# Opening two chunks of a feed-forward block side by side, without a plain first chunk, in a macaron encoder

## Chip, cores and metric

One core of a Trainium2 chip runs the whole program. The metric is the device time of one execution in microseconds (us), as the median of several runs; before the change it is 2751.84 us. A profile of one execution shows when each engine works: PE (TensorE, matmuls and transposes), DVE (VectorE), ACT (ScalarE), POOL (GpSimd, here mostly an issuer of DMAs that add to their target) and SP (SyncE, issuer of the loads).

## The reference

Two layers run over 768 tokens of 1024 features (a batch of 512 and one of 256). Each layer is a macaron block: half a feed-forward network, a token mixer, half a feed-forward network.

```python
def rmsnorm(x, g):
    xf = x.astype(F32)
    y = xf * lax.rsqrt(jnp.mean(xf * xf, axis=-1, keepdims=True) + NORM_EPS)
    return (y * g.astype(F32)).astype(x.dtype)

def swiglu_ffn(x, w1, w2):
    gate, up = jnp.split(x @ w1, 2, axis=-1)
    return (jax.nn.silu(gate) * up) @ w2
...
        x = x + 0.5 * swiglu_ffn(rmsnorm(x, norm_g[li, 0]), ffn_w1[li, 0], ffn_w2[li, 0])
        h = rmsnorm(x, norm_g[li, 1])
...
        x = x + mix
        x = x + 0.5 * swiglu_ffn(rmsnorm(x, norm_g[li, 2]), ffn_w1[li, 1], ffn_w2[li, 1])
    return rmsnorm(x, final_norm_g)
```

The first layer's mixer is a gated linear recurrence (hgrn), the second's is windowed attention (swa). The hidden width of the feed-forward network is 2816, that is 22 chunks of 128.

## The kernel before

**Stages.** f0, hgrn, f1, f2, swa, f3: four feed-forward blocks f0 to f3 and two mixers. f1 starts out of hgrn's output projection, f2 directly out of f1's last down product, f3 out of swa's projection.

**Numbers.** The matmuls work on pairs of high and low parts (`hi`, `lo`, of a type of fewer bits): a product of two values is three matmuls, hi by hi, hi by lo, lo by hi. The part `hi` is a cast by ACT, `lo` is the difference by DVE (`split`, lines 238 and 239 for weights, 383 and 384 for activations).

**Tokens in two halves.** The 768 tokens are two halves of 384 (H). A norm works on a block of 128 tokens: ACT squares and sums it (L433), takes the root (L434), DVE takes the reciprocal and scales the block (L435, L436). `turn` then transposes three blocks at a time by PE (L475) and ACT copies the result out of PSUM with the norm's weight (L478). There are four such groups of transposes for each norm: two parts of the features (part 0 and 1) for each half of the tokens. The quarters are called b00, b10, b01, b11 (part, half).

**A chunk.** The up projection of one chunk (gate and up columns) by all tokens is either plain, `up_plain`: 2 x 2 x 8 products, 96 matmuls of 128x384; or a Strassen pair, `up_pair`: seven products p1 to p7 of four steps, 84 matmuls. In a pair each product has its own operand: p1 takes b01, p2 b11, p3 b10, and p4 to p7 take the sums s4, s3, s2, s1 of the quarters, which DVE makes (`first_sum`, `up_sums`) and ACT and DVE split. Each product also has its own weight out of the four raw blocks of 128x512 of a chunk: single blocks for p1, p2, p4, and sums for the others, made partly by POOL's adding DMAs (`into`, L160) in separate `s3` tiles.

**The opening of a block.** While a norm's second half is still being made, a block of f1 to f3 starts with chunk 0 plain and chunk 1 as `opened_pair`, which takes its products in the order p7, p3, p1, p2, p6, p5, p4 and yields control so that the plain matmuls of the second half stand between. Block f0 has two plain chunks. From chunk 2 on every chunk is `up_pair`.

**Order and buffers.** Weights are planned in a queue: SP loads raw blocks into four `wr` slots (`load_next`, L175), ACT and DVE split them (`stage_next`), and `ahead` does so one product before PE needs it, within a bound of staged tiles (`GATED` while a block's first operands are missing). Work that belongs to the norms (`turn`, the sums) is put in `deferred` and run by `run_later` at set places. Each engine executes its own queue in order: an instruction that waits holds up all that stand behind it. A last down product (`down_last`) adds PE's results to x and calls the next norm for each block as soon as its two column halves are ready.

## Time and profile before

| | value |
|---|---|
| median of 3 runs | 2751.84 us (2751.36 to 2751.96) |
| profiled execution | 2752.12 us |
| its span in the trace | 2750.3 us |
| POOL busy | 470.8 us (17%) |
| DMA, mean | 124 GB/s |
| matmuls of a pair's products (L669) | 6972 |
| f1's opening | from 1022.20 us in the span |
| f2's opening | from 1508.17 us |
| f3's opening | from 2258.71 us |

The span is what the trace covers; the execution's own time is some 2 us more. Busy time of an engine over the whole span is an average over stages. Of PE, a row's duration overlaps the next, so the spacing of starts gives its pace. The chain of waits is followed back from the last instruction to what released each.

### The profile page before, as it was taken

What the parts mean: (1) busy time and instruction counts of PE and PEld (TensorE: products, weight loads), DVE (VectorE), ACT (ScalarE), POOL (GpSimd) and SP (SyncE); (2) the same over time, 40 slices, a digit from 0 to 9 for tenths busy, and PEclk for the clock granted to TensorE, in tenths of its full rate; (3) what the DMA queues carried; (4) which work ended last, traced back from release to release, by engine and by line L of the source; (5) the groups of instructions that cost most, each with busy time, mean ns of one, the idle gap of its engine ahead of it and who ended that gap; (6) DMA issues with size and microseconds to landing.
All of it is one profiled execution on the core that took longest, in us unless ns stands there. A gap on an engine that the chain in (4) does not pass through costs nothing.

```text
span 2750.3 us, 41122 instructions
## 1 busy us (share of the span) xinstructions
PE 2736.6 (99%) x15071; PEld 2544.4 (93%) x15071; DVE 2194.6 (80%) x3790; ACT 1407.9 (51%) x2664; POOL 470.8 (17%) x534
## 2 busy tenths in 40 slices
PE   9999999999999999999999999999999999999998
PEld 9999999989999889999998999999888889999997
DVE  8788788767877789788878987887847869788877
ACT  6344444634454676444455643444458855444444
POOL 1111121200000111211121121112005621211120
PEclk9999999999999999999999999999999999999999
DMA  6554556741122755655455565545424435655453
GB/s 176 128 127 115 124 145 166 223 144 38 40 56 68 199 132 126 146 134 129 117 135 138 115 149 129 130 115 142 130 74 114 87 76 121 142 134 131 115 135 111
DMA packets 363002, 340.70 MB, mean 124 GB/s; under 512 B 15320, under 2 KB 275376, under 8 KB 362800
## 3 DMA queue, kind: packets, MB, share of 16 engines
q1 hardware_dynamic: 306944, 227.18, 28.0%
q0 software_dynamic: 51552, 97.41, 20.4%
q10 hardware_dynamic: 4304, 13.49, 1.4%
q8 instruction: 118, 1.93, 0.3%
q14 instruction: 84, 0.69, 0.1%
HBM read 228.45 MB, written 15.73 MB: 89 GB/s over the span
## 4 chain that ended last, share of the span: by engine, by line
PE 94%; DMA 2%; DVE 1%; ACT 1%; issue 1%; POOL 0%; SPq 0%; ACTq 0%; POOLq 0%; DVEq 0%
PE ps L669 44%; PE ps L778 17%; PE ps L811 6%; PE ps L379 5%; PE ps L380 5%; PE ps L378 5%; PE ps L994 5%; PE ps L1057 3%; PE ps L475 1%; PE ps L1162 1%; PE ps L1676 1%; PE ps L1138 1%; PE ps L1638 0%; PE ps L1639 0%; PE ps L1688 0%
## 5 line engine op out<-in xcount | busy, mean ns | idle before, releaser
L669 PE MATMUL ps<-big,w 128*128 128x384 f32 x6972 | 1213.2, 334 | 0.0
L669 PEld LDWEIGHTS ps<-big,w 128*128 128x128 f32 x6972 | 1209.5, 188 | 1.4
L238 ACT CAST w<-wr 128x512 fp32r<-128x512 f32 (+1 forms) x615 | 430.0, 706 | 663.4 <-PE ps L669 336.0
L239 DVE TENSOR_TENSOR w<-wr,w 128x512 fp32r<-128x512 f32 (+1 forms) x541 | 435.8, 809 | 141.8 <-ACT w L238 115.1
L778 PE MATMUL ps<-w,big 128*128 128x512 f32 x2016 | 461.1, 390 | 0.0
L778 PEld LDWEIGHTS ps<-w,big 128*128 128x128 f32 x2016 | 376.6, 188 | 80.5 <-ACT big L383 2.7
L160 POOL DMA_DIRECT2D s<-wr x135 | 118.8, 890 | 1228.1 <-DVE wr L245 278.4
L841 DVE SCALAR_TENSOR_TENSOR x<-ps,x 128x512 f32<-128x512 f32 x420 | 273.0, 683 | 11.5 <-PE ps L811 11.2
L384 DVE TENSOR_TENSOR big<-tA,big 128x384 fp32r<-128x384 f32 x308 | 187.9, 621 | 20.9 <-ACT big L383 20.6
L160 POOL DMA_DIRECT2D wr<-wr x115 | 101.7, 885 | 537.9 <-DVE big L384 142.9
L383 ACT CAST big<-tA 128x384 fp32r<-128x384 f32 x308 | 152.8, 514 | 75.5 <-DVE tA L703 29.8
L378 PE MATMUL ps<-big,w 128*128 128x384 f32 x544 | 187.3, 345 | 0.1
L379 PE MATMUL ps<-big,w 128*128 128x384 f32 x544 | 183.1, 337 | 0.2 <-DVE big L455 0.2
L380 PE MATMUL ps<-big,w 128*128 128x384 f32 x544 | 182.6, 336 | 0.3 <-DVE w L384 0.3
L994 PE MATMUL ps<-w,big 128*128 128x512 f32 x756 | 178.2, 393 | 0.1
L811 PE MATMUL ps<-w,big 128*128 128x512 f32 x756 | 174.7, 391 | 0.9 <-DVE x L841 0.9
L811 PEld LDWEIGHTS ps<-w,big 128*128 128x128 f32 x756 | 141.0, 188 | 31.1 <-DVE x L841 2.0
L994 PEld LDWEIGHTS ps<-w,big 128*128 128x128 f32 x756 | 140.3, 188 | 29.0 <-DVE w L384 0.6
L239 POOL TENSOR_TENSOR w<-wr,w 128x512 fp32r<-128x512 f32 x74 | 107.4, 1452 | 81.0 <-ACT w L238 73.4
L245 DVE TENSOR_TENSOR wr<-wr,wr 128x512 f32<-128x512 f32 (+1 forms) x120 | 114.8, 956 | 0.4 <-DVE w L239 0.4
L384 DVE TENSOR_TENSOR w<-wr,w 128x1024 fp32r<-128x1024 f32 (+1 forms) x74 | 88.2, 1198 | 30.3 <-ACT w L383 29.1
L383 ACT CAST w<-wr 128x1024 fp32r<-128x1024 f32 (+1 forms) x74 | 75.7, 1029 | 70.1 <-PE ps L379 35.7
(251 smaller groups left out, 3698.5 us busy)
## 6 DMA issues: line engine op xcount, KB each, us to landing
wr<-in_ffn_w_dram SPq DMA_DIRECT2D x254, 512.0 KB, 4.0
s<-wr POOLq DMA_DIRECT2D x135, 256.0 KB, 4.7
s<-in_ffn_w_dram SPq DMA_DIRECT2D x126, 256.0 KB, 3.2
wr<-wr POOLq DMA_DIRECT2D x86, 256.0 KB, 4.1
wr<-in_hg_w_in_dram SPq DMA_DIRECT2D x32, 512.0 KB, 3.9
wr<-wr POOLq DMA_DIRECT2D x29, 512.0 KB, 4.7
spill<-x ACTq DMA_DIRECT2D x12, 512.0 KB, 4.0
kept<-big POOLq DMA_DIRECT2D x8, 768.0 KB, 6.1
```

Source lines behind the costliest of these rows:

```text
L238: nc.scalar.copy(h, src)
L239: (eng or nc.vector).tensor_sub(l, src, h.bitcast(F32))
L378: nc.tensor.matmul(out, a[0], b[0], start=first, stop=False)
L379: nc.tensor.matmul(out, a[0], b[1], start=False, stop=False)
L380: nc.tensor.matmul(out, a[1], b[0], start=False, stop=last)
L383: self.last_hi = self.nc.scalar.copy(hi, src).ins
L384: self.last_lo = self.nc.vector.tensor_sub(lo, src, hi.bitcast(F32)).ins
L669: self.nc.tensor.matmul(ps, a[x], b[y], start=first and k == 0 and i == 0, stop=k == 3 and i == 2, skip_group_check=True,)
L778: nc.tensor.matmul(ps, a[x], w[y], start=name == chain and kp == 0 and q == 0, stop=kp == 1 and q == 2, skip_group_check=True,)
L811: nc.tensor.matmul(ps, a[x], w[y], start=name == chain and k == 0 and q == 0, stop=k == 2 and q == 2, skip_group_check=True,)
L841: self.nc.vector.scalar_tensor_tensor(x, ps, c, x, ALU.mult, ALU.add)
L994: nc.tensor.matmul(ps, x[:, sl], y, start=fresh and k == 0 and q == 0, stop=k == 3 and q == 2, skip_group_check=True,)
```

## The change

Three settings and the code of the opening change, in f1, f2 and f3 alone:

- No plain chunk (`PLAIN` 0). Chunks 0 and 1 are both opened pairs and run side by side, product by product: p3 of chunk 0, p3 of chunk 1, then p7, p1, p2, p6, p5, p4 likewise.
- Half 0 is turned part 1 first, since p3 needs b10 and s1 needs both; b00 itself is no longer split, since no product takes it.
- The weights of both chunks are planned as one entry ("open") of eight raw blocks of 128x512 in four `wr` slots. The second chunk's two sum tiles are in a tile of the activations' pool (`big`), since there are only two `s3` tiles. Up to eight staged weight tiles may wait for the first operands (`GATED` 4).
- In the last down product ahead of a norm, `half_square` squares one half of a block's columns (of the first three blocks after p2, of the others after p5) and puts the sum through a scale and the epsilon; `norm_block` then squares the other half only and takes the root with the first as its bias.

```diff
-PLAIN = {"f0": 2, "f1": 1, "f2": 1, "f3": 1}
-GATED = 2
+PLAIN = {"f0": 2, "f1": 0, "f2": 0, "f3": 0}
+GATED = 4
...
-OPEN = ("p1", "p2", "p7", "p3", "p6", "p5", "p4")
+OPEN = ("p3", "p7", "p1", "p2", "p6", "p5", "p4")
...
+        if how == OPEN:
+            both = [self.quad_steps((key[0], i), raws[2 * i : 2 * i + 2], srcs[2 * i : 2 * i + 2], how) for i in range(2)]
+            steps = [step for pair in zip(*both) for step in pair]
+            inuse = lambda left: 4 if left > 5 else 3 if left == 5 else min(left, 2)
+            self.loaded.append((steps, inuse))
+            return
...
+        spot = self.big([P, 2, 512]) if order == OPEN and key[1] else None
         for i, src in enumerate(three):
-            t = self.wp.tile([P, 512], F32, tag="s3", name=self.name("s3"), bufs=2)
+            if spot is None:
+                t = self.wp.tile([P, 512], F32, tag="s3", name=self.name("s3"), bufs=2)
+            else:
+                t = spot[:, i]
...
+    def half_square(self, b, c):
+        nc = self.nc
+        xn, r = self.big([P, D]), self.stat(1)
+        sl = slice(c * 512, c * 512 + 512)
+        nc.scalar.activation(xn[:, sl], self.x[b][:, sl], AF.Square, accum_out=r)
+        nc.scalar.activation(r, r, AF.Identity, bias=self.eps, scale=1.0 / D)
+        self.ready[b] = xn, r, slice(512 - c * 512, D - c * 512)
+
     def norm_block(self, b, vector=False):
         nc = self.nc
+        if b in self.ready:
+            xn, bias, sl = self.ready.pop(b)
+            r = self.stat(1)
+            nc.scalar.activation(xn[:, sl], self.x[b][:, sl], AF.Square, accum_out=r)
+            nc.scalar.activation(r, r, AF.Sqrt, bias=bias, scale=1.0 / D)
...
-        if half == 0 and part == 0:
+        if half == 0 and part == int(row in (2, 3, 5)):
...
-                self.put(f"b{part}{half}", kp, self.tn[(part, half)][:, kp])
+                if part or half or row < 2:
+                    self.put(f"b{part}{half}", kp, self.tn[(part, half)][:, kp])
...
-        self.later(lambda: self.turn(half, 0, row), lambda: self.turn(half, 1, row))
+        parts = (1, 0) if not half and row in (2, 3, 5) else (0, 1)
+        self.later(*(lambda part=part: self.turn(half, part, row) for part in parts))
...
-        pair = self.opened_pair(tag, 1)
-        pss = self.up_plain(tag, 0, 0, iter(()), ((3,), (0, 3)))
-        next(pair)
-        ts[0] = self.gated(pss, self.last_hi, self.last_lo)
+            return ts
+        pairs = [self.opened_pair(tag, j) for j in range(2)]
+        self.run_later()
+        for name in OPEN:
+            for j, pair in enumerate(pairs):
+                out = next(pair)
+                if (name, j) in (("p7", 0),):
+                    self.run_later()
+                elif (name, j) == ("p7", 1):
+                    self.run_later(len(self.deferred))
+                if name == "p4":
+                    for half, t in out:
+                        ts[2 * j + half] = t
+                        if (j, half) != (0, 1):
+                            put(f"b{j}{half}", t, 0)
...
+                elif name == "p5":
+                    self.half_square(HB + i, 1)
+                elif name == "p2" and next_row is not None:
+                    self.half_square(i, 0)
```

How the instructions stand on three engines where f2 opens, before and after (numbers behind a name tell tiles apart; they differ between the two programs).

POOL's adding DMAs ahead of f2's first products, before. The chunk of the opened pair has the raw blocks `wr_1894` and `wr_1895` and the two sum tiles `s3_1896` and `s3_1897`:

```order
L160 DMA s3_1896_13425<-wr_1894_13421 128x512
L160 DMA s3_1897_13428<-wr_1894_13421 128x512
L160 DMA wr_1895_13423<-wr_1895_13423 128x512
L160 DMA s3_1897_13428<-wr_1895_13423 128x512
L160 DMA wr_1894_13421<-wr_1895_13423 128x512
```

The same place after. The first chunk has `wr_1903`, `wr_1904` and two `s3` tiles, the second `wr_1905`, `wr_1906` and both halves of `big_1909`:

```order
L161 DMA s3_1907_13458<-wr_1903_13450 128x512
L161 DMA s3_1908_13461<-wr_1903_13450 128x512
L161 DMA wr_1904_13452<-wr_1904_13452 128x512
L161 DMA s3_1908_13461<-wr_1904_13452 128x512
L161 DMA big_1909_13466<-wr_1905_13454 128x512 x2
L161 DMA wr_1906_13456<-wr_1906_13456 128x512
L161 DMA big_1909_13466<-wr_1906_13456 128x512
```

The chain of adds stands there twice now; that of the second chunk is last.

ACT's queue at the first transposes of f2's norm, before (`ps_1930` to `ps_1934` hold them; `w_1925` and `w_1937` are the plain chunk's gate and up weights):

```order
L434 ACTIVATE stat_1923_13609<-stat_1923_13609,eps_78 128x1
L383 CAST w_1924_13614<-big_1876_13251 128x512
L383 CAST w_1925_13617<-wr_1892_13417 128x1024
L383 CAST w_1937_13681<-wr_1893_13419 128x1024
L478 ACTIVATE big_1931_13658<-ps_1930_13654,cols_121 128x384
L478 ACTIVATE big_1931_13658<-ps_1932_13660,cols_121 128x384
L478 ACTIVATE big_1931_13658<-ps_1933_13665,cols_121 128x384
L478 ACTIVATE big_1931_13658<-ps_1934_13670,cols_121 128x384
L383 CAST big_1935_13675<-big_1931_13658 128x2x384
```

The same place after (`w_1940` and `w_1941` are p3's weights of the two chunks):

```order
L249 CAST w_1940_13666<-s3_1908_13461 128x512
L452 ACTIVATE stat_1938_13658<-stat_1938_13658,stat_1917_13518 128x1
L442 ACTIVATE big_1943_13683,stat_1944_13684<-x_1253_8824 128x512
L442 ACTIVATE big_1946_13698,stat_1947_13699<-x_1254_8826 128x512
L443 ACTIVATE stat_1944_13684<-stat_1944_13684,eps_78 128x1
L443 ACTIVATE stat_1947_13699<-stat_1947_13699,eps_78 128x1
L442 ACTIVATE big_1949_13713,stat_1950_13714<-x_1255_8828 128x512
L249 CAST w_1941_13669<-big_1909_13466 128x512
L443 ACTIVATE stat_1950_13714<-stat_1950_13714,eps_78 128x1
L506 ACTIVATE big_1952_13721<-ps_1951_13717,cols_121 128x384
L506 ACTIVATE big_1952_13721<-ps_1953_13723,cols_121 128x384
```

Ahead of the evacuations there stood casts of whole raw blocks; now two casts of summed tiles stand there, that of `w_1941` out of the last tile that POOL's adds complete, and the three half squares of the other token half.

PE's queue where f2's products begin, before (the last down matmuls, then the plain chunk's first; `w_1925` is chunk 0's gate weight):

```order
L811 MATMUL ps_1929_13643<-w_1913_13559,big_1805_12759 128x512
L811 MATMUL ps_1929_13643<-w_1924_13614,big_1882_13337 128x512 x3
L378 MATMUL ps_1957_13775<-big_1935_13675,w_1925_13617 128x384
L379 MATMUL ps_1957_13775<-big_1935_13675,w_1925_13617 128x384
L380 MATMUL ps_1957_13775<-big_1935_13675,w_1926_13618 128x384
```

The same place after (`big_1956` and `big_1957` are the split b10, `big_1972` is the split s1):

```order
L854 MATMUL ps_1948_13702<-w_1939_13663,big_1893_13370 128x512 x3
L710 MATMUL ps_1974_13838<-big_1956_13738,w_1940_13666 128x384 x6
L710 MATMUL ps_1974_13838<-big_1957_13741,w_1940_13666 128x384 x6
L710 MATMUL ps_1977_13856<-big_1956_13738,w_1941_13669 128x384 x6
L710 MATMUL ps_1977_13856<-big_1957_13741,w_1941_13669 128x384 x6
L710 MATMUL ps_1983_13882<-big_1972_13831,w_1958_13744 128x384
```

Twenty-four matmuls on b10 come first, and the operand of the twenty-fifth is already a sum of two quarters; before, the plain chunk took four quarters one after the other.

## The prediction, made before the change was run

> **What bounds the kernel now.** I read the page's busy table first, then its chain that ended last, then the windows and timelines of the three stages that the edit touches: the openings of f1, f2 and f3, that is the first two chunks' products with the transposes between them.

> ```profile
> PE 2736.6 (99%) x15071; PEld 2544.4 (93%) x15071; DVE 2194.6 (80%) x3790; ACT 1407.9 (51%) x2664; POOL 470.8 (17%) x534
> PE 94%; DMA 2%; DVE 1%; ACT 1%; issue 1%; POOL 0%; SPq 0%; ACTq 0%; POOLq 0%; DVEq 0%
> ```

> Over the whole span PE is the bound: 99% busy, 94% of the chain. ACT at 51% looks idle. That average hides the stages in question, so here are two windows of f2's opening and one each of f1's and f3's (PE, PEld, DVE, ACT, POOL busy us, then clock, DMA share, GB/s):

> ```profile
> 1034.00:1046.00 12.00, 12.00 (x71) 12.00 (x71) 12.00 (x16) 11.97 (x21) 2.01 (x3) 1.00 0.60 132
> 1508.00:1520.00 12.00, 11.95 (x77) 11.30 (x76) 11.42 (x18) 12.00 (x24) 3.50 (x4) 1.00 0.62 107
> 1520.00:1532.00 12.00, 12.00 (x71) 12.00 (x70) 12.00 (x16) 11.97 (x21) 3.53 (x4) 1.00 0.55 125
> 2270.00:2282.00 12.00, 12.00 (x71) 12.00 (x70) 12.00 (x16) 11.97 (x21) 3.53 (x4) 1.00 0.55 128
> ```

> In the openings three engines are full at once: PE, and the two that feed it, DVE and ACT, both near 12.00 of 12. PE is fed just in time there, so less matmul work brings time only if the feeders' work shrinks or comes earlier. The granted clock is 1.00, so PE's rate is fixed.

> When each opening begins and ends (timeline of PE and chain; a row of the chain is start, length, what, count):

> ```profile
> 1022.20 0.33 PE L378 MATMUL ps<-big,w 128*128 128x384 f32 x1
> 1048.19 37.56 PE ps L669 x216
> 1508.17 0.33 PE L378 MATMUL ps<-big,w 128*128 128x384 f32 x1
> 1534.32 37.44 PE ps L669 x216
> 2258.71 0.33 PE L378 MATMUL ps<-big,w 128*128 128x384 f32 x1
> 2284.81 37.44 PE ps L669 x216
> ```

> One 128x384 matmul takes 37.44/216 = 0.1733 us. Each last row ends (1085.75, 1571.76, 2322.25) with the 168 matmuls of chunks 2 and 3, 29.1 us, so the openings end at 1056.6, 1542.6 and 2293.1: each lasts 34.4 us. In it stand 96 + 84 = 180 matmuls (31.2) and 24 transposes (12 take 1.47 with the tail of the last, some 1.23 by their starts, so 2.46): 33.7. **Some 0.75 us of small stalls** are in each opening already.

> **The change, part by part.**

> *Fewer matmuls.* Chunk 0 as a pair has 84 instead of 96: 12 x 0.1733 = 2.08 us for each block. The new opening at full pace is 168 x 0.1733 + 2.46 = 31.6, which is 34.4 - 31.6 = 2.84 under the old one. For three blocks: **-8.5 us**, if nothing waits.

> *The feeders.* The sums s1 to s4, until now wanted after 96 plain matmuls, are wanted at once: in the new order p7 (operand s1) comes second, p6 (s2) before p2. The rows of f2 that price a feeder's step (ACT, then DVE, then f1's and f3's first evacuation):

> ```profile
> 1499.88 1.99 ACT L478 ACTIVATE big<-ps,cols 128x384 f32<-128x384 f32 x4 [0.18 <-PE ps L475]
> 1501.74 1.58 ACT L383 CAST big<-big 128x768 fp32r<-128x768 f32 x2
> 1514.68 1.15 ACT L238 CAST w<-s 128x512 fp32r<-128x512 f32 x2
> 1502.62 1.83 DVE L384 TENSOR_TENSOR big<-big,big 128x768 fp32r<-128x768 f32 x2 [0.88 <-ACT big L383]
> 1504.37 0.69 DVE L239 TENSOR_TENSOR w<-wr,w 128x512 fp32r<-128x512 f32 x1
> 1507.72 0.75 DVE L436 TENSOR_SCALAR big<-x,stat 128x1024 f32<-128x1024 f32 x1
> 1016.81 2.00 ACT L478 ACTIVATE big<-ps,cols 128x384 f32<-128x384 f32 x4 [2.95 <-PE ps L475]
> 2251.86 1.99 ACT L478 ACTIVATE big<-ps,cols 128x384 f32<-128x384 f32 x4 [1.47 <-PE ps L475]
> ```

> Call A0 the start of the first evacuation and t0 PE's first product. DVE starts its first difference at A0 + 2.7 (1502.62 against 1499.88). Counted off the changed program's order, it then has up to the low part of s2 15 steps of 768 columns (0.87 each by their starts), 8 to 10 weight differences of 512 (0.6), three 1024-column scalings (0.67), two to four residual adds (0.6) and reciprocals (0.3): 13.05 + 6 + 2 + 1.2 + 0.3 = 22.6 us. So s2 stands at A0 + 25.3. ACT's queue to the same place is about as long (16 evacuations 7.4, nine casts 6.6, ten weight casts 5.3, copies, squares and roots 4): 23. PE wants s2 after p3, p7 and p1 of both pairs: 72 x 0.1733 + 2.46 = 15.0 us after t0. It therefore waits 25.3 - 15.0 = 10.3 us less t0 - A0. That distance is 1022.20 - 1016.81 = 5.4 in f1 and 2258.71 - 2251.86 = 6.85 in f3; in f2 it becomes 5.9 (next part). **Stalls: f1 4.9, f2 4.4, f3 3.5, together +12.8.** Bounds: 0 if the queues hold nothing back (before, PE lost only 0.75 there), and 1.5 us more for each opening if ACT's and DVE's queues take turns instead of overlapping, some 17 in all.

> *A wait that ACT did not have there.* The second pair's p3 weight is the sum of four raw blocks. Its last term is added by a GpSimd DMA, and p3 is now the first product. The chain in f2, before:

> ```profile
> 1491.93 0.37 SPq L175 DMA_DIRECT2D wr<-in_ffn_w_dram  x1
> 1494.17 1.83 POOL L160 DMA_DIRECT2D s<-wr  x2 [26.66 <-DVE x L841]
> 1496.39 1.38 POOL L160 DMA_DIRECT2D wr<-wr  x1 [0.38 <-DVE stat L435]
> 1501.52 0.86 POOL L160 DMA_DIRECT2D s<-wr  x1 [3.76 <-issue]
> DMA to landing us min/median/max: 2.5/4.3/10.4
> s<-wr POOLq DMA_DIRECT2D x135, 256.0 KB, 4.7
> ```

> SP can load the last raw block only at 1491.93, when the last down quad frees the slot (the new pair's last block takes the same slot); the add inside it and the add into the sum follow, 5.1 us apart. The last is issued at 1501.52 and lands, at 4.7 us, at 1506.2. Before, nobody wanted it until ACT's casts at 1514.68. Now ACT's cast of it stands in front of a half square's scaling and of **every** evacuation of the transposes (in f1 of the third block's root as well). So the first evacuation starts at 1506.2 + 0.55 + 0.2 = 1506.95. Behind it: the second transposes (PE at 1502.75) need the banks that these evacuations empty, so they start at 1507.4 instead.

> ```profile
> 1502.75 1.47 PE L475 MATMUL ps<-ident_r,big 128*128 128x128 f32 x12
> 1012.32 0.88 POOL L160 DMA_DIRECT2D s<-wr  x1 [3.09 <-DMA wr<-wr]
> 1016.60 0.60 PE ps L475 x5
> ACT w L238 <- DMA wr<-wr: 61.6, 26, 3.9
> ```

> PE loses 1507.4 - 1502.75 = **4.7 us in f2**, and t0 - A0 becomes 1508.17 + 4.7 - 1506.95 = 5.9. In f1 the same add is issued at 1012.32 and lands at 1017.0; cast 0.55, root 0.3, reciprocal 0.15 and scaling 0.75, with some 0.4 of handing over, bring the third block's transposes to 1019.2, where PE stood ready at 1016.6 and the products behind them start as much later: **2.6 us in f1**. In f3 swa's end gives the loads some 15 us more: nothing. Sum of holds **+7.3**. Ends of the range: with adds of 2.5 us instead of 4.7 it is 0.5 + 2.5 = 3; with one of 10.4 it would be 8 + 10 = 18. ACT has waited for such adds 26 times, at most 3.9 us, so I stay at the median.

> [...]

> *Half squares* (ends of f0, f1, f2). Each 1024-column square becomes two of 512 plus a small bias; ACT does about 0.3 us more for each block, half of it earlier. At f0 to hgrn and f2 to swa PE had matmuls left to do and no wait ended on that square: 0, at worst 1 us late each, at best 0.5 us won each. I take 0.3.

> **The sum.** -8.5 + 12.8 + 7.3 + 0.3 = +11.9 on the profiled execution's 2752.12 (its span is 2750.3, the rest lies around it; the median of the runs shown is 2751.84, 0.3 lower): **2764 us**.

> **The rivals.**
> - *B, the openings stall but ACT's cast finds its data.* Should the last add land before ACT gets there (the scheduler's order frees the slot earlier, or ACT is late anyway), only -8.5 + 12.8 remains: 2756.4. For it: the four raws are now four loads of one kind on SP. Against: the row at 1491.93 is set by a slot, not by SP.
> - *C, the other side: faster.* The feeders keep up and only the saved matmuls count: 2752.1 - 8.5 = 2743.6. It decides at t0 - A0 = 10.3 us or a feeder's queue shorter by 4 to 5 us; then PE is the only bound, as 99% says. Against: 12.00 and 11.97 in the windows. [...]
> - *D, longer waits.* Adds at 6 to 7 us instead of 4.7, in two places (+4), and one more on the weights of p7 (its sum lies on the same chain, +2): 2770.
> - *E, the openings break even* (stalls of 8.5, two thirds of the sum) and the holds stay: 2752.1 + 7.3 = 2759.4.

> **How the numbers follow.** Forecast 0.50, B 0.20, C 0.08, D 0.12, E 0.10. A measurement of this kernel tells about 0.2%, 5.5 us, from no change: faster is below 2746.3 (C, 0.08), the same up to 2757.3 (most of B and a little of E, 0.17), slower above it (0.75). The range reaches from 2750 (holds at 3, openings' stalls at 3.5) to 2771 (D); only C and an extreme add lie outside.

> **What would show it.** In the changed profile: 36 matmuls of 128x384 fewer; an ACT wait for a GpSimd add, on the cast of the weight just ahead of the first evacuations, in f1 and f2 and not in f3; PE's second transposes in f2 some 5 us behind the matmuls ahead of them; PE gaps before p7 and p6 of each opening, released by DVE or ACT; the openings of f3 about 35 us long. Wrong it would be if the openings take 31.6 us, or if PE's gaps end on a weight load or at the norms ahead of hgrn and swa.

## The result, and the profile after

The changed kernel takes 2781.72 us (median of 4 runs, 2778.22 to 2786.33) against 2751.6: a ratio of 1.011 (95% interval 1.0097 to 1.0122). It is **slower by about 30 us**, where the forecast was 12 slower and the range ended at 2771. The execution in the profile is the longest of the four, 2786.33 us with a span of 2784.2; its stages add up to +34, not +30.

First the page after: busy time, and the share of each engine in the chain that ended last.

```profile
PE 2745.6 (99%) x15035; PEld 2546.2 (91%) x15035; DVE 2200.3 (79%) x3817; ACT 1420.3 (51%) x2736; POOL 484.7 (17%) x549
PE 91%; DVE 3%; DMA 2%; ACT 1%; issue 1%; POOL 0%; SPq 0%; ACTq 0%; POOLq 0%; DVEq 0%
```

15071 - 15035 = 36 matmuls went, as meant. PE still reads 99%, so this table shows nothing of the loss: its busy time rose from 2736.6 to 2745.6 us although it has less to do. The chain shows some of it: PE's share is 91% instead of 94%, and DVE's 3% instead of 1%.

To find the place I compared four moments of each block in both traces (starts in the timeline of PE, us): the first transposes of the norm, the first product, the first matmul of the first down product, the first product behind it.

| block | | first transposes | first product | first down | behind it |
|---|---|---|---|---|---|
| f1 | before | 1011.06 | 1022.20 | 1085.59 | 1114.47 |
| | after | 1011.30 | 1026.84 | 1095.22 | 1127.63 |
| f2 | before | 1499.35 | 1508.17 | 1571.60 | 1600.22 |
| | after | 1512.57 | 1528.59 | 1596.09 | 1625.92 |
| f3 | before | 2247.48 | 2258.71 | 2322.09 | 2350.70 |
| | after | 2274.96 | 2286.19 | 2352.24 | 2384.97 |

The differences of neighbouring columns give what each stretch costs more than before, beside the prediction's terms:

| stretch | f1 | f2 | f3 | predicted |
|---|---|---|---|---|
| up to the first product (hold) | +4.4 | +7.2 | 0.0 | 2.6, 4.7, 0 |
| opening and chunks 2, 3 | +5.0 | +4.1 | +2.7 | 2.1, 1.6, 0.7 |
| first down product | +3.5 | +1.2 | +4.1 | 0 |

With 1.8 us inside swa these make 34. The first two rows lie where they were looked for, but larger; the third was not expected at all.

**What a gap costs twice.** f2's hold after: POOL's last add into p3's weight, ACT's queue, PE's, and four windows (the column behind POOL's is the granted clock).

```profile
1516.95 0.88 POOL L161 DMA_DIRECT2D big<-wr  x1 [4.76 <-issue]
1520.28 0.62 ACT L249 CAST w<-big 128x512 fp32r<-128x512 f32 x1 [3.96 <-issue]
1521.00 1.98 ACT L506 ACTIVATE big<-ps,cols 128x384 f32<-128x384 f32 x4
```

```profile
1521.61 1.85 PE L503 MATMUL ps<-ident_r,big 128*128 128x128 f32 x9 [4.41 <-ACT big L506]
1523.11 5.64 PE L854 MATMUL ps<-w,big 128*128 128x512 f32 x18
1516.00:1520.00 4.00, 1.20 (x7) 0.76 (x5) 0.00 (x0) 0.32 (x2) 0.88 (x1) 1.00 0.44 83
1520.00:1524.00 4.00, 2.39 (x11) 1.97 (x12) 1.56 (x3) 3.72 (x8) 0.00 (x0) 0.80 0.00 0
1524.00:1528.00 4.00, 4.00 (x15) 3.13 (x15) 4.00 (x7) 4.00 (x10) 0.23 (x1) 0.77 0.10 28
1528.00:1532.00 4.00, 4.00 (x24) 3.88 (x23) 3.24 (x7) 3.76 (x11) 1.50 (x2) 1.00 0.50 103
```

ACT stands idle 3.96 us ahead of its cast of p3's weight, which stands ahead of the first evacuation; PE waits 4.41 us for the bank. The trace names no releaser for ACT's wait (`issue`). That it is POOL's add is read from the tile (the second chunk's sum is in `big`) and the time, 3.3 us behind the add's issue; experiments 6 and 10 test it. Behind the gap 18 matmuls take 5.64 us, and the clock is 0.80 and 0.77 for two windows. Before the change the same 18 took 4.36:

```profile
1503.97 4.36 PE L811 MATMUL ps<-w,big 128*128 128x512 f32 x18
```

The trace's clock reads 0.50 from 1522.4 for 3.41 us and 1.00 on both sides. If PE is busy throughout, that is 3.4 x 0.5 = **1.7 us for one episode**, an estimate (the 18 matmuls alone show 1.28 of it). The profiled execution has six of them (f1's hold, opening and first down product, f2's hold, f3's opening and first down product): 10.2 us. Before the change there was none in these stretches (1.00 in all of them).

In f1 the same kind of add delays the third block's root and scaling, and PE waits for that block:

```profile
1019.03 0.77 PE L503 MATMUL ps<-ident_r,big 128*128 128x128 f32 x5 [2.53 <-DVE big L464]
```

**The wait in the middle of an opening.** ACT, POOL and PE in f1 after:

```profile
1031.39 0.94 POOL L161 DMA_DIRECT2D wr<-wr  x1
1036.18 0.62 ACT L249 CAST w<-wr 128x512 fp32r<-128x512 f32 x1 [2.56 <-DMA wr<-wr]
1037.58 1.22 PE L710 MATMUL ps<-big,w 128*128 128x384 f32 x3 [2.58 <-ACT big L394]
```

p6's weight is a sum too. Its add may start only when p1's weight is split, and it is a GpSimd DMA as well: issued at 1031.39, and ACT's cast starts at 1036.18. The cast of s1's second half stands behind it on ACT, and PE waits for that.

**The first down product.** After and before, from top to bottom the add of the down weight (after only), ACT's cast of it, and PE:

```profile
1087.87 0.86 POOL L161 DMA_DIRECT2D wr<-wr  x1 [10.23 <-ACT ps L735]
1093.42 2.00 ACT L249 CAST w<-wr 128x1024 fp32r<-128x1024 f32 x2 [5.85 <-DMA wr<-wr]
1101.38 26.41 PE L821 MATMUL ps<-w,big 128*128 128x512 f32 x108 [1.88 <-DVE x L888]
```

```profile
1081.80 1.05 ACT L238 CAST w<-wr 128x1024 fp32r<-128x1024 f32 x1 [3.85 <-DMA wr<-wr]
1085.59 29.04 PE L778 MATMUL ps<-w,big 128*128 128x512 f32 x126
```

Before, the cast started 3.8 us ahead of the first down matmul and nothing came of its wait; after, 1.8 us ahead (1095.22 - 1093.42), DVE's queue behind it is late, and PE stops for DVE's first residual adds.

### The profile page after: what moved, and what is told of

It reads as the page before. It is cut to its first block, busy times and chain, and to the rows that moved or that the text cites. A ratio compares the mean times of both kernels' runs of the same rounds, so it can differ in the third digit from the quotient of the medians.

```text
span 2784.2 us, 41223 instructions
## 1 busy us (share of the span) xinstructions
PE 2745.6 (99%) x15035; PEld 2546.2 (91%) x15035; DVE 2200.3 (79%) x3817; ACT 1420.3 (51%) x2736; POOL 484.7 (17%) x549
## 4 chain that ended last, share of the span: by engine, by line
PE 91%; DVE 3%; DMA 2%; ACT 1%; issue 1%; POOL 0%; SPq 0%; ACTq 0%; POOLq 0%; DVEq 0%
PE ps L710 42%; PE ps L821 16%; PE ps L854 6%; PE ps L1036 6%; PE ps L389 4%; PE ps L391 4%; PE ps L390 4%; PE ps L1099 3%; DMA wr<-wr 1%; PE ps L1204 1%; PE ps L1718 1%; PE ps L503 1%; DVE big L395 1%; DMA wr<-in_ffn_w_dram 1%; PE ps L1180 1%
## 5 line engine op out<-in xcount | busy, mean ns | idle before, releaser
L710 PE MATMUL ps<-big,w 128*128 128x384 f32 x7224 | 1264.8, 335 | 10.3 <-ACT big L394 6.9
L710 PEld LDWEIGHTS ps<-big,w 128*128 128x128 f32 x7224 | 1255.1, 188 | 16.8 <-ACT big L394 9.3
L249 ACT CAST w<-wr 128x512 fp32r<-128x512 f32 x630 | 438.3, 704 | 679.4 <-PE ps L710 316.9
L250 DVE TENSOR_TENSOR w<-wr,w 128x512 fp32r<-128x512 f32 (+1 forms) x556 | 447.3, 808 | 154.3 <-ACT w L249 132.9
L389 PE MATMUL ps<-big,w 128*128 128x384 f32 x448 | 154.6, 346 | 0.0
L390 PE MATMUL ps<-big,w 128*128 128x384 f32 x448 | 150.6, 336 | 0.1
L391 PE MATMUL ps<-big,w 128*128 128x384 f32 x448 | 150.2, 335 | 0.3 <-DVE w L395 0.3
L738 DVE TENSOR_TENSOR tA<-tA,ps 128x384 f32<-128x384 f32 x80 | 44.1, 551 | 82.1 <-PE ps L710 82.1
L256 DVE TENSOR_TENSOR wr<-wr,wr 128x512 f32<-128x512 f32 (+1 forms) x120 | 108.6, 905 | 0.1
L395 DVE TENSOR_TENSOR w<-wr,w 128x1024 fp32r<-128x1024 f32 (+1 forms) x68 | 80.7, 1192 | 29.4 <-ACT w L394 29.1
## 6 DMA issues: line engine op xcount, KB each, us to landing
s<-wr POOLq DMA_DIRECT2D x135, 256.0 KB, 4.7
s<-in_ffn_w_dram SPq DMA_DIRECT2D x126, 256.0 KB, 3.1
wr<-wr POOLq DMA_DIRECT2D x92, 256.0 KB, 4.2
big<-in_ffn_w_dram SPq DMA_DIRECT2D x26, 256.0 KB, 5.4
```

Source lines behind the costliest of these rows:

```text
L249: nc.scalar.copy(h, src)
L250: (eng or nc.vector).tensor_sub(l, src, h.bitcast(F32))
L389: nc.tensor.matmul(out, a[0], b[0], start=first, stop=False)
L390: nc.tensor.matmul(out, a[0], b[1], start=False, stop=False)
L391: nc.tensor.matmul(out, a[1], b[0], start=False, stop=last)
L395: self.last_lo = self.nc.vector.tensor_sub(lo, src, hi.bitcast(F32)).ins
```

## The experiments

All were timed beside the kernel before. "Stretches" are read as in the table above.

**1 to 3: the two adds.** `p3early` loads each opened chunk's second raw block first and puts the adds in the order that this asks for:

```diff
-        for src in srcs:
+        for at in (1, 3, 0, 2) if how == OPEN else range(len(srcs)):
...
         self.into(a21, a22)
         if order == OPEN:
             self.into(s3[1], a21)
+            self.into(s3[1], a11)
+            self.into(s3[0], a11)
```

> The changed kernel, but of each chunk opened side by side the second raw block is loaded first, so that only one add (not two) stands between the last raw load and p3's weight. Theory W (ACT is held in front of the first evacuations by that add, and PE pays the gap and then some 3.4 us of half clock behind it): the holds go in f1 (PE wait of 2.5 us at the third block's transposes) and f2 (4.4 us at the second transposes) and with them the half clock behind each, together 9 to 12 us: about 2770. Rival R (ACT and DVE are simply full in the openings): the time saved in front comes back as a wait for s1 and s2; at most 3 us faster, 2779 or more.

Measured 2779.32 us (ratio 1.0084 to 1.0114). f1's hold is +2.8, though PE still waits 2.56 us there: only the half clock behind the wait is missing. f2's is +9.5: ACT now waited 7.2 us for an add of the first chunk (`ACT w L253 <- DMA s<-wr` in the waits), since POOL took the adds in another order and the last load still waits for a slot. The edit left f1's wait and moved f2's, it took neither away; it tells nothing between the theories.

`p6dve`:

```diff
-            add = {"second": lambda: self.into(a11, a21)}
+            add = {"second": lambda: nc.vector.tensor_add(a11, a11, a21)}
```

> The changed kernel, but the add that makes p6's weight (second raw part onto the first, once p1's weight is split) is done by DVE instead of a GpSimd DMA. Theory W: ACT's cast of that weight waits for the DMA in the middle of each opening (2.6 us in f1, some 4 to 5 us in f2 and f3) and everything behind it on ACT comes late; without it the openings of f1, f2, f3 are 3 to 4 us shorter each, less 1.2 us for two DVE adds each: about 2773. Rival R (feeders full): DVE has 1.2 us more to do in each opening, up to 3.6 us slower: 2782 to 2785.

Measured 2779.37 us (1.0086 to 1.012). The openings are +3.4, +1.9 and +1.3 instead of +5.0, +4.1 and +2.7: 1.6, 2.2 and 1.4 us less, although DVE has more to do. In f1 and f3 the changed kernel's openings have one half-clock episode each and those of `p6dve` have none, so these two differences are about the clock behind the wait (1.7 us); in f2 neither kernel has one in the opening, and the 2.2 us are wait alone. ACT's cast of that weight in f1 now starts without a wait:

```profile
1032.02 0.62 ACT L249 CAST w<-wr 128x512 fp32r<-128x512 f32 x1
1034.36 0.84 ACT L394 CAST big<-big 128x768 fp32r<-128x768 f32 x1 [1.72 <-DVE big L566]
```

The next wait on ACT is one for DVE's sum, so the add was a wait on top of full feeders: both theories hold a part. The whole time fell by 2 us only, within the changed kernel's spread; the stretches carry the verdict.

`p3p6` is both edits at once.

> Both edits at once (second raw block first, p6's add by DVE). Theory W: the two add up, about 17 to 20 us off the changed kernel, 2762 to 2765, what is left being the waits at the first down product and the feeders' own work. Rival R: no more than 3 us off, 2779 or more.

Measured 2776.13 us (1.0071 to 1.0101): openings +3.6, +0.3, +1.3, f2's hold +9.7. As `p3early` left the hold in place, neither number was met.

**4 and 5: the raw slots, and their control.** `raw5`, with `slots20` as the same kernel with four raw slots:

```diff
-RAWBUFS = 4
-SLOTS = 21
+RAWBUFS = 5
+SLOTS = 20
```

> The changed kernel with five raw-weight slots instead of four, and 20 instead of 21 slots of the activations' pool to make room. Theory S (the opening holds its four raw slots until p6 and p4 are split, so the loads of the chunks and of the first down product behind it run late): the waits at the first down products (3.5, 1.2 and 4.1 us with their half clock) go, and the last raw block before each opening is loaded some us earlier, which shortens the holds of f1 and f2 as well: 2766 to 2772. Rival: the loads have slack, the late thing at the down product is DVE's queue alone; then 2780 or more, slower if the pool's slot was needed.

> The changed kernel with 20 instead of 21 slots in the activations' pool, the raw slots still four: the control of the five-slot run. If the pool's slot matters neither way, it stays within the changed kernel's own spread, 2778 to 2786, and what five raw slots brought (11 us) is theirs. If fewer pool slots by themselves changed the order for the better, 2775 or less.

`raw5`: 2770.29 us (1.0052 to 1.0082), `slots20`: 2784.74 (1.0102 to 1.0133). So the 11 us are the fifth slot's. The first down products are at -0.2, +0.1 and +0.1, and f1's hold at 0.0. POOL and ACT of `raw5` at f1's first down product:

```profile
1080.13 0.86 POOL L161 DMA_DIRECT2D wr<-wr  x1 [5.95 <-issue]
1089.93 1.06 ACT L249 CAST w<-wr 128x1024 fp32r<-128x1024 f32 x1 [3.15 <-PE ps L710]
```

The add is issued 11.6 us ahead of the first down matmul (1091.77) instead of 7.4, and ACT's cast waits for PE, no longer for a DMA. f2's hold stays at +6.9: there the load of the last raw block is issued at 1498.26, 7.4 us ahead of the first transposes, as before the change and in the changed kernel, and two adds follow. The openings of `raw5` are +5.7, +0.8 and +2.7.

`raw5p6` joins the fifth slot and `p6dve`.

> The changed kernel with five raw slots and p6's add by DVE, nothing left out. Theory W with S: the two parts add up, 11.4 us (raw slots) and some 4 to 5 us (p6's wait in the three openings) off the changed kernel, 2765 to 2767, the rest above the kernel before being f2's hold on p3's last add (about 5 us with half clock) and the openings. Rival: they share the same waits and do not add, 2769 or more.

Measured 2769.45 us (1.005 to 1.008): 0.8 less than `raw5`, so they do not add in the whole time. By stretches f1's opening (+3.0) and f3's (+1.3) got shorter; f2's hold (+8.3, a wait of 5.80 us with two half-clock episodes, where `raw5` has 4.53 us and two), f2's opening (+1.7) and swa (+3.5 instead of +2.3) got longer.

**6: the last add.** `noadd` leaves it out:

```diff
-        if order == OPEN:
-            self.into(s3[1], a21)
```

> The changed kernel with the last add of p3's weight left out in each opened pair (the sum a21 + a22 does not go into it, so p3 is computed with part of its weight). Theory W: this add alone holds ACT in front of the first evacuations; without it the stretch from the first transposes to the first product, 4.4 us longer than before the change in f1 and 7.2 in f2, is within 1 us of before in both, with no half clock there; 9 to 11 us off, about 2771. Rival R: the feeders are full, the time comes back in the openings (now 5.0, 4.1 and 2.7 us longer than before), which grow by most of it; 2778 or more.

Measured 2771.89 us (1.0057 to 1.0087), 9.8 less than the changed kernel. ACT in f1: all casts of weights ahead of the evacuations are done by 1012.6, and the first evacuation waits for the transposes alone.

```profile
1012.00 0.62 ACT L247 CAST w<-big 128x512 fp32r<-128x512 f32 x1
1015.91 2.00 ACT L504 ACTIVATE big<-ps,cols 128x384 f32<-128x384 f32 x4 [1.91 <-PE ps L501]
```

The hold is 0.0 in f1 and +4.6 in f2, where PE now waits 2.79 us for a residual add of the last down product, with half clock behind. The time did not come back: the openings are +4.3, +1.7, +2.7, no longer than in the changed kernel. Theory W holds in f1; in f2 it holds for a part. With five slots it holds for all of it: `raw5p6` above and `clean` below differ in this add alone, and f2's hold is +8.3 with it and 0.0 without, the whole time 8.4 us apart.

**7: the clock.** `warm` fills the gap with work that changes no value:

```diff
+            again = 4 if (row, half, part) == (3, 0, 1) else 1
-            for i in range(HB):
+            for i in [i for _ in range(again) for i in range(HB)]:
```

> The changed kernel, but the first twelve transposes of f2's norm are done four times over (the same values into the same places), which fills some 3.7 us of the gap in which PE waits for its second transposes. Theory C (the granted clock falls to half for 3.4 us because PE was idle before): the clock stays at 1.00 behind this gap, and from the first transposes to the first product of f2 it takes 5.5 us more than before the change instead of 7.2, though PE did 3.7 us more work. Rival: the clock falls for another reason (or the extra work delays the evacuations): half clock there as before, 7.2 or more. On the whole time: 2780, within the spread of the changed kernel.

Measured 2781.08 us (1.0088 to 1.0122). PE of `warm` with two windows of its clock:

```profile
1522.33 0.55 PE L504 MATMUL ps<-ident_r,big 128*128 128x128 f32 x3 [1.17 <-ACT big L507]
1522.63 4.38 PE L855 MATMUL ps<-w,big 128*128 128x512 f32 x18
1518.00:1522.00 4.00, 2.30 (x13) 1.38 (x11) 2.25 (x4) 3.72 (x8) 0.00 (x0) 1.00 0.01 3
1522.00:1526.00 4.00, 3.67 (x18) 3.08 (x19) 3.31 (x5) 3.29 (x7) 0.87 (x1) 1.00 0.41 97
```

The clock stays at 1.00 and the 18 matmuls take 4.38 us instead of 5.64: theory C holds for this gap, in the one execution profiled (the last section has the other gaps). The stretch still is +7.2, not 5.5, as ACT put casts between the evacuations in this order, and the second transposes ended late.

**8 and 9: the half squares.** `halfonly` is the kernel before with `half_square` alone, `nohalf` the changed kernel without it.

```diff
-                elif name == "p5":
-                    self.half_square(HB + i, 1)
-                elif name == "p2" and next_row is not None:
-                    self.half_square(i, 0)
```

> The kernel before with the half squares alone. My step said 0.3 us in all. If the half squares cost what the changed kernel shows between f2's first down product and f3's first transposes (1.8 us more than before), it is 2753 to 2754; if they win time at the ends of f0, f1 and f2, 2750 or less.

> The changed kernel without the half squares. In the kernel before they changed nothing, so by my theory nothing here either: within 2 us of the changed kernel, 2780 to 2784. Rival: standing on ACT's queue ahead of f2's evacuations they cost, or squaring in halves brings the first transposes of f2 earlier; then 4 us or more to one side, seen between f2's first transposes and its first product.

`halfonly`: 2751.8 us (0.9991 to 1.0009): nothing. `nohalf`: 2785.82 (1.0107 to 1.0141), some 4 us more than the changed kernel, but the two intervals overlap. Its profile has f1's hold at +7.0 (a wait of 4.67 us instead of 2.53) and eight half-clock episodes; f1's norm has no half squares, so that wait is of another order of the queues. Whether they save anything in the changed kernel stays open.

**10 to 12: what is left without weight waits.** `clean` joins `raw5`, `p6dve` and `noadd`; `cleanpool` gives the low parts of p1's and p2's weights in the openings to GpSimd; `cleanlow` leaves out those of p7, p1 and p2.

```diff
# cleanpool
-            split(name, own[name], nc.gpsimd if spare and name == "p5" else None)
+            split(name, own[name], nc.gpsimd if spare and name == "p5" or order == OPEN and name in ("p1", "p2") else None)
# cleanlow
                 nc.scalar.copy(h, src)
+                if order == OPEN and name in ("p7", "p1", "p2"):
+                    lo = hi
+                    continue
                 (eng or nc.vector).tensor_sub(l, src, h.bitcast(F32))
```

> All three at once: five raw slots, p6's add by DVE, p3's last add left out. Theory W with S: nothing waits for a weight any more. The holds and the waits at the first down products are gone in all three blocks, no half clock is left, and what remains is the feeders' own work in the openings: f1 +3, f2 +1.5, f3 +1.3 against before, so 2757 to 2761. If the feeders had room (the faster rival of the prediction) the openings would be 2.84 shorter each, 2744 to 2746. Rival R: 2768 or more, the openings 5 us longer each.

> The kernel without weight waits (five raw slots, p6's add by DVE, p3's last add left out), with the low parts of p1's and p2's weights of the opened pairs made by GpSimd: 2.4 us of differences off DVE in each opening. Theory F (what is left in the openings is DVE's and ACT's own work up to s2): each opening ends 0.8 to 2 us earlier, 2755 to 2759. Rival: ACT alone is the limit, or GpSimd's 1.4 us for each part makes the weights late: the openings stay as they are or grow, 2761 or more.

> The kernel without weight waits (five raw slots, p6's add by DVE, p3's last add left out), which in addition leaves out the low parts of the weights of p7, p1 and p2 in the opened pairs (the high part is taken twice): six differences of 0.6 us, 3.6 us of DVE's work before s2, go from each opening, and nothing is given to GpSimd. Theory F (what is left in the openings, 2.9, 3.2 and 1.4 us more than before, is DVE's work up to s2): each opening 2 to 3 us shorter, to about 0 or below, 2753 to 2757. Rival: ACT's queue of some 23 us sets it, then at most 1 us each, 2758 to 2761.

`clean`: 2761.01 us (1.002 to 1.0046). No hold, no wait at a first down product; openings +2.9, +3.2 and +1.4, the second with one half-clock episode (1.7). PE's waits in f1's opening are those of the feeders, ahead of p7 and then behind 72 matmuls, which is where the prediction had PE want s2:

```profile
1027.71 0.45 PE L708 MATMUL ps<-big,w 128*128 128x384 f32 x1 [1.24 <-ACT big L392]
1041.48 0.61 PE L708 MATMUL ps<-big,w 128*128 128x384 f32 x2 [1.32 <-ACT big L392]
1042.75 1.49 PE L708 MATMUL ps<-big,w 128*128 128x384 f32 x7 [0.66 <-DVE big L393]
```

`cleanpool`: 2774.36 us (1.0067 to 1.0096); the openings grow to +7.9, +6.6, +5.7, PE waits 1.77 and 2.25 us for a scaled block that DVE brings late. It met its rival and says nothing of DVE's own load. `cleanlow`: 2755.87 us (1.0006 to 1.0025), openings +0.3, -0.2, +1.0:

```profile
1027.45 0.45 PE L711 MATMUL ps<-big,w 128*128 128x384 f32 x1 [0.57 <-ACT big L395]
1040.49 1.83 PE L711 MATMUL ps<-big,w 128*128 128x384 f32 x9 [0.65 <-DVE big L396]
```

With 3.6 us taken off DVE, f1's opening lost 2.7 us and f2's 3.4 (1.7 of it the clock); f3's only 0.3. Theory F is shown for f1; f2 without the clock falls short of the 2 to 3 us expected, and f3's is what the rival expected.

No kernel here that computes everything beat the one before. With nothing waiting for a weight it is still 9 us slower: 5.8 us are in the openings, 1.7 are f2's half clock, 2.4 are in swa, and some 1 us was won elsewhere.

## Why the prediction was wrong, by its steps

- **The sign was right, and two of the three places.** "-8.5, if nothing waits": 36 matmuls went, and `clean` shows that the feeders alone give back more than that (its openings are 5.8 us longer than before without the clock, so 14.3 went to waits, where the prediction had 12.8).
- **The sum, in parts that don't overlap.** Of the 34 us in the profiled execution 10.2 are half clock. Without it the holds are 8.2 (forecast 7.3), the openings 8.4 (4.3), the first down products 5.4 (0), swa 1.8 (0). So of the 22 us that the forecast of 11.9 lacks, nearly half is the clock, a quarter the first down products and a fifth the openings.
- **The holds: right in mechanism; that the waits' sizes fit so well is in part luck.** 2.6 and 4.7 us were forecast for f1 and f2; PE waited 2.53 and 0.56 + 4.41. f3 has none, as forecast. But the add took at most 3.8 us in f1 and 3.3 in f2 to ACT's cast, not 4.7. In f2 it was issued 4.4 us behind the first transposes, where the sum took the 2.2 of the trace before; in f1 DVE did two weight differences of 0.69 us ahead of the third block's scaling that the sum left out. These errors nearly cancel. The holds came out at 4.4 and 7.2 for another reason:
- **The step that failed first, and the largest: "The granted clock is 1.00, so PE's rate is fixed."** It was read from a trace that lists no wait of PE (none above 0.15 us) in these stretches. In the changed kernel PE waited 2.53, 2.58 and 1.88 us in f1, 4.41 in f2, 1.11 with 0.45 and 2.33 in f3, and with each of these six the clock reads 0.50 for 3.41 us; six times the estimated 1.7 us is 10.2 of the 34. The prediction put no price on it.
- **The opening's stalls.** The term "+12.8" took the weights as there whenever ACT reached them. p6's add was not counted: 1.6, 2.2 and 1.4 us by `p6dve`, of which those in f1 and f3 are the half clock behind the wait and are in the 10.2 as well. What the step did count, the feeders' work, fits: with no weight waited for the openings are +2.9, +1.5 (less the clock) and +1.4, where 2.1, 1.6 and 0.7 were forecast, and DVE had 1.2 us more to do for p6. By `cleanlow` DVE's queue sets f1's, and f2's at least in part, as the sum of 25 us against ACT's 23 had it; for f3 this isn't shown.
- **A term that was missing: the first down products**, 8.8 us in all. The step on the loads asked where the openings' own raws come from, and not who gets the slots next. The opened chunks hold all four slots until p6 and p4 are split, so what stands behind has to wait for one. `raw5` took 3.7, 1.1 and 4.0 us of it away. Part of those 8.8 is half clock: f1's and f3's stretches have an episode each, counted in the 10.2 too.
- **Half squares:** 0.3 forecast, 0.0 by `halfonly`.
- **The range** left no room for it: rival D had "longer waits" and one more weight, 6 us beyond the forecast, and no price for the clock or the slots.

Open: swa is 1.2 to 3.7 us longer in the changed kernels, with single waits of about 1 us for ACT and DVE; nothing in it was changed, and `halfonly` doesn't show it. The four kernels with 3.0 us or more there (`cleanlow`, `raw5p6`, `slots20`, `cleanpool`) have one half-clock episode each in swa (in `cleanlow` from 2159.5 us on, for 3.4 us), the others none; what brings the rest isn't known. Nor is it settled why f2's hold and opening are longer in `raw5p6` than in `raw5`.

## What to carry to other kernels

Ahead of a stretch that is fed just in time, a new wait costs its own length and then the clock behind it: here each of nine waits of PE from 2.60 to 5.94 us in five traces had a fall of the clock to 0.50 in it or behind it, an estimated 1.7 us for 3.41 us of it, where one of 2.59 us in `p6dve` had none. Put a price on such a gap, and look for it in the windows behind it, as the busy share doesn't show it (99% before and after). When work is moved to the front of a stage, list each weight that it needs with its last add, and ask who gets the buffers next: here the slots held longer cost as much as the wait that was seen (`raw5` is 11.4 us below the changed kernel, `noadd` 9.8). Averages say nothing of an opening in which three engines are full; here 36 fewer matmuls brought nothing (`clean`'s openings are 5.8 us longer than before without the clock), and f1's got 2.7 us shorter when 3.6 us were taken off DVE.

## What the runs showed of the hardware that was not expected

The half-clock episodes of the changed kernel's trace last 3.41 us each (an estimated 1.7 us lost in each), and in `nohalf`, `slots20`, `raw5p6` and `cleanpool` 3.4, 6.8 or 10.2 us, but there isn't one behind every gap. In these five traces, from 980 to 1140, 1470 to 1650 and 2240 to 2420 us, each of the nine waits of PE from 2.60 us up (to 5.94) has a fall of the clock in it or within 3.4 us behind it; of the six from 2.25 to 2.58 us five have one, and one, of 2.25 us in `cleanpool`, lies in half clock already. In `p6dve` a wait of 2.59 us ahead of f1's third block left the clock at 1.00; in `clean` two short ones, 1.30 and 0.65 us, brought it down in f2, and 1.32 and 0.66 us in f1 did not:

```profile
1018.48 0.77 PE L503 MATMUL ps<-ident_r,big 128*128 128x128 f32 x5 [2.59 <-DVE big L464]
1018.00:1022.00 4.00, 3.51 (x22) 2.97 (x23) 2.62 (x5) 3.15 (x6) 0.00 (x0) 1.00 0.23 66
```

```profile
1529.38 0.62 PE L708 MATMUL ps<-big,w 128*128 128x384 f32 x2 [1.30 <-ACT big L392]
1530.65 0.69 PE L708 MATMUL ps<-big,w 128*128 128x384 f32 x1 [0.65 <-DVE big L393]
1530.00:1534.00 4.00, 3.35 (x12) 3.35 (x12) 4.00 (x6) 4.00 (x8) 2.65 (x3) 0.57 0.40 67
```

That may be why the changed kernel's runs spread over 8 us (2778.22 to 2786.33, mean clocks 0.998 to 0.996) where those of the kernel before stay within 3; it wasn't tested by itself.
